# Both rope products of a projection half in one VectorE operation of 1024 columns, with the sine reached by a backward step

## The chip, the cores and the metric

The kernel runs on the 8 cores of one Trainium2 chip, as one program for all of them; each core computes 2048 of the 16384 tokens. The metric is the time of the slowest core, in microseconds (us). Before the change it was 1009.27 us, the median of 3 runs (1008.91 to 1009.8).

One property of this program decides how its runs have to be compared. In most runs some pairs of cores (0 and 1, 2 and 3, 4 and 5, 6 and 7) run with TensorE at a granted clock of 0.81 (46.1 to 209.0 us in the profiled run before); the other pairs don't, also on the same die (in the profiled run before, cores 0 and 1 ended at 1005 us with the stretch, cores 2 and 3 at 989 to 991 us without). Which pairs it is changes from run to run. A core that has this stretch ends about 16 us later and has a mean clock near 0.957, one that doesn't has about 0.983. The profiled runs show the stretch itself; in the other runs I tell the two kinds apart by the mean clock. I call them **lower-clock** and **higher-clock** cores. The time of a run is that of its lower-clock cores, unless there are none, which happened in 9 of the 40 later runs of the kernel before (993 to 995 us, where nearly all others had 1006 to 1010). Those runs make ratios of whole runs noisy (they also make an ordinary run of 1008.5 us count as slow, being over 1.5% above the fastest), so the experiments below compare lower-clock cores with lower-clock cores and higher-clock cores with higher-clock ones, always with the kernel before in the same rounds on the same chip. Cores over 1040 us, in the few runs of a much slower state (1042 to 1169 us, mean clock 0.806 to 0.929), are left out.

## The reference, cut to what matters

```python
def apply_rope(t):                       # t: (B, S, H, 64)
    ...                                  # cos, sin by position and by 32 frequencies
    t1, t2 = tf[..., :half], tf[..., half:]
    out = jnp.concatenate([t1 * cos - t2 * sin, t2 * cos + t1 * sin], axis=-1)

def reference(x, ...):
    h = rms_norm(x, g_pre_mix[l])
    proj = h @ w_in[l]                   # q, k, v, pool input, gates
    q = apply_rope(q)
    k = apply_rope(k)
    # dilated window attention in three groups of heads, pooling branch, gated merge,
    # output projection, then a SwiGLU feed-forward layer
```

Rope needs four products for each projection: with a = t1 and b = t2, it needs a·cos and b·sin (subtracted), and a·sin and b·cos (added).

## The kernel before

Weights are permuted so that all first halves of four heads come out of one group of eight matmuls and all second halves out of the next. They land in two neighbouring PSUM banks. VectorE makes the products with a table from SBUF; GpSimd adds or subtracts and writes bf16.

```python
tabs = P.ring("tab", [128, 2, 512], F32, ...)        # row 0 cosine, row 1 sine; two buffers
rt = P.ring("rt", [128, 2, 512], F32, ..., False)    # products; two buffers
any2, fill2 = pairs([0, 2, 4, 6]), pairs([4, 6])     # pairs of PSUM banks
# ... cut ...
def rope(ring, wa, wb, rhs, tn, dst_a, dst_b, view, n=512, t0=0):
    tb = tab(tn)
    b = ring.new()
    cos, sin = tb[:, 0, t0:t0 + n], tb[:, 1, t0:t0 + n]
    mm8(b[:, 0, 0:n], wa, rhs)
    mm8(b[:, 1, 0:n], wb, rhs)
    for dst, fa, fb, op in ((dst_a, cos, sin, ALU.subtract), (dst_b, sin, cos, ALU.add)):
        t = rt.new()
        dve.tensor_tensor(out=t[:, 0, 0:n], in0=b[:, 0, 0:n], in1=fa, op=ALU.mult)
        dve.tensor_tensor(out=t[:, 1, 0:n], in0=b[:, 1, 0:n], in1=fb, op=ALU.mult)
        pool.tensor_tensor(out=dst, in0=view(t[:, 0, 0:n]), in1=view(t[:, 1, 0:n]), op=op)
```

The kernel doesn't fix the order of its instructions by hand. It records every operation as a node with its dependencies, then a list scheduler orders the five engines' queues with the kernel's own prices, and only then are the instructions and semaphore waits written out. The prices that matter here:

```python
def op_cost(eng, method, outs, ins, kw):             # us
    # ... cut ...
    if eng == "vector":
        # ... cut: reciprocal, and all-bf16 operations ...
        return 0.12 + (0.00170 if strided else 0.00110) * n
```

So a product of 512 columns is priced at 0.683 us and one of 1024 at 1.246 us. There are 30 projections with rope, 29 of 512 columns and one of 128: 120 products before.

The softmax here doesn't subtract the row's maximum and nothing guards it: scores larger than these inputs give would overflow.

## Time and profile before

| | before |
|---|---|
| time, median | 1009.27 us |
| profiled run, by core | 988.9 to 1007.7 us |
| PE busy (slowest core) | 93% |
| VectorE busy | 379.4 us, 509 instructions |
| products (the tiles rt) | 120, from 27 to 319 us |

In the profile, PE is TensorE, DVE is VectorE, ACT is ScalarE, POOL is GpSimd. The first lines are the cores' spans and mean granted clocks.

```profile
core 2: 990.8 us, clock 0.984
...
core 5: 1007.7 us, clock 0.957
```

Core 2 is a higher-clock core here, core 5 a lower-clock one. From the page of core 5: busy time, share and number of instructions of each engine, and below it the granted TensorE clock in 40 slices of 25 us.

```profile
PE 941.1 (93%) x5520; PEld 483.0 (48%) x5520; DVE 379.4 (38%) x509; ACT 349.2 (35%) x558; POOL 364.9 (36%) x366
...
PEclk9888888899999999999999999999999999999997
```

TensorE is the limit of the whole, and VectorE matters only where TensorE waits for it. The groups of products follow: operation, output and inputs, shape, count, then the busy time, the mean length of one in ns, and how long the engine was idle before them and for whom.

```profile
L608 DVE TENSOR_TENSOR rt_72_114<-ps,tab_71_113 128x512 f32<-128x512 f32 x30 | 20.3, 685 | 24.7 <-PE ps L608 22.5 <-POOL q_1_65_107 L608 1.5 <-POOL k_34_76 L608 0.6
...
L608 DVE TENSOR_TENSOR rt_73_115<-ps,tab_71_113 128x512 f32<-128x512 f32 x30 | 19.8, 681 | 3.7 <-POOL q_1_65_107 L608 2.5 <-POOL k_34_76 L608 0.7 <-POOL q_33_75 L608 0.5
...
L608 DVE TENSOR_TENSOR rt_72_114<-ps,tab_70_112 128x512 f32<-128x512 f32 x28 | 18.7, 686 | 16.7 <-PE ps L608 9.4 <-ACT PT_75_117 L608 2.9 <-POOL k_34_76 L608 2.6
L608 DVE TENSOR_TENSOR rt_73_115<-ps,tab_70_112 128x512 f32<-128x512 f32 x28 | 18.3, 679 | 1.7 <-POOL q_33_75 L608 1.0 <-POOL k_34_76 L608 0.7
```

How a projection runs shows in the timeline (start, length, engine, operation, count; in brackets the idle time before it):

```profile
143.81 2.01 PE L610 MATMUL ps<-hTh_69,wk_67_109 128*128 128x512 bf16 x7
...
144.16 0.69 DVE L608 TENSOR_TENSOR rt_72_114<-ps,tab_71_113 128x512 f32<-128x512 f32 x1 [2.53 <-PE ps L608]
...
144.77 0.68 DVE L608 TENSOR_TENSOR rt_73_115<-ps,tab_71_113 128x512 f32<-128x512 f32 x1
...
145.65 0.44 PE L608 MATMUL ps<-hTh_69,wk_67_109 128*128 128x512 bf16 x1
...
146.20 0.69 DVE L608 TENSOR_TENSOR rt_72_114<-ps,tab_71_113 128x512 f32<-128x512 f32 x1 [0.74 <-PE ps L608]
...
146.80 0.68 DVE L608 TENSOR_TENSOR rt_73_115<-ps,tab_71_113 128x512 f32<-128x512 f32 x1
147.03 2.17 POOL L608 TENSOR_TENSOR k_0_61_103<-rt_72_114 128x512 bf16<-128x512 f32 x1 [4.79 <-DVE rt_72_114 L608]
```

The second half's matmuls run from 143.81 to 146.09. In that time VectorE already makes both products of the first half. Two products in a row start 0.60 us apart although each lasts 0.68 us or more. GpSimd begins 0.94 us after the second half ended, and the last read of the bank pair ends at 147.48, 1.39 us after it.

The table by stretches (start:end, length, busy time of PE, its weight loads, DVE, ACT, POOL with counts, granted clock, DMA share, GB/s) of core 5:

```profile
46.00:205.00 159.00, 153.12 (x1223) 103.62 (x1221) 90.34 (x134) 93.69 (x157) 78.05 (x58) 0.81 0.44 111
205.00:285.00 80.00, 74.61 (x708) 47.86 (x707) 57.83 (x80) 40.09 (x62) 49.45 (x37) 0.99 0.19 41
285.00:300.00 15.00, 11.49 (x108) 6.04 (x105) 10.36 (x17) 6.15 (x8) 8.79 (x7) 0.89 0.36 53
300.00:330.00 30.00, 26.49 (x152) 12.07 (x153) 21.07 (x26) 12.23 (x15) 22.82 (x22) 0.94 0.43 65
```

The clock of 0.81 is the long stretch of the lower-clock cores.

### The profile page before, as it was taken

Reading aid. Unit: us, or ns where it says so; the run is one execution under the profiler, and the core shown is the slowest. Engines: PE = TensorE matmul, PEld = TensorE weight load, DVE = VectorE, ACT = ScalarE, POOL = GpSimd, SP = SyncE. Lnnn points to the kernel's source line nnn. Section 1 sums busy time; section 2 is a strip of 40 time slices with the busy share of each in tenths; the row PEclk is TensorE's granted clock in tenths of the full one; section 3 lists DMA queues with packets and bytes.
Section 4 is the critical chain, followed back from the end, with each engine's and each line's share of the span. In section 5 each row is a group of like instructions: output and inputs, shape, how many; then the busy total and the mean of one; then the engine's idle time right before and its main releaser. Section 6 shows DMA issues by size and latency. Waiting matters only on the chain.

```text
span 1007.7 us, 15210 instructions; the slowest of 8 cores (988.9 to 1007.7 us)
## 1 busy us (share of the span) xinstructions
PE 941.1 (93%) x5520; PEld 483.0 (48%) x5520; DVE 379.4 (38%) x509; ACT 349.2 (35%) x558; POOL 364.9 (36%) x366
## 2 busy tenths in 40 slices
PE   2789999998988999999899999999999999999992
PEld 1356686665743444444444444444444444444441
DVE  5667625658767434332544121121112112111111
ACT  4696425653634434422774111111111111110110
POOL 1526643455757352533885111111322000001332
PEclk9888888899999999999999999999999999999997
DMA  8967710140024633640877665663234344430321
GB/s 233 286 168 230 165 36 2 43 84 2 23 54 62 117 53 61 158 74 14 265 239 207 113 116 106 108 124 79 89 126 125 66 81 83 66 61 21 105 84 42
DMA packets 30777, 105.01 MB, mean 104 GB/s; under 512 B 3952, under 2 KB 3952, under 8 KB 30704
## 3 DMA queue, kind: packets, MB, share of 16 engines
q0 software_dynamic: 14432, 45.65, 26.9%
q1 hardware_dynamic: 15984, 58.33, 17.3%
q8 instruction: 45, 0.74, 0.3%
q14 instruction: 28, 0.23, 0.1%
q10 hardware_dynamic: 288, 0.06, 0.0%
HBM read 132.90 MB, written 16.78 MB: 149 GB/s over the span
## 4 chain that ended last, share of the span: by engine, by line
PE 82%; DVE 4%; POOL 4%; issue 4%; ACT 2%; DMA 1%; SPq 0%; POOLq 0%; DVEq 0%; ACTq 0%
PE ps L610 73%; PE ps L608 10%; DMA xst_40_82<-xo 1%; DVE PT_75_117 L608 1%; ACT xsb_53_95 L608 1%; POOL x1b_103_145 L608 1%; POOL x1b_102_144 L608 1%; DVE PT_74_116 L608 1%; DVE rt_73_115 L608 1%; POOL x1b_101_143 L608 0%; DVE zT_134 L608 0%; POOL x1b_104_146 L608 0%; POOL q_33_75 L608 0%; DVE val_67 L608 0%; DVE x1b_102_144 L608 0%
## 5 line engine op out<-in xcount | busy, mean ns | idle before, releaser
L610 PE MATMUL ps<-wdna_155,ffT_154 128*128 128x512 bf16 x512 | 115.7, 379 | 0.0
L610 PE MATMUL ps<-hT_68,wgu_109_151 128*128 128x512 bf16 x420 | 100.4, 379 | 0.0
L610 PE MATMUL ps<-hT_68,wgu_110_152 128*128 128x512 bf16 x420 | 100.4, 379 | 0.0
L610 PE MATMUL ps<-hT_68,wgu_111_153 128*128 128x512 bf16 x392 | 93.7, 379 | 0.0
L610 PEld LDWEIGHTS ps<-wdna_155,ffT_154 128*128 128x128 bf16 x512 | 50.1, 98 | 60.4
L610 PEld LDWEIGHTS ps<-hT_68,wgu_109_151 128*128 128x128 bf16 x420 | 41.0, 98 | 49.3
L610 PEld LDWEIGHTS ps<-hT_68,wgu_110_152 128*128 128x128 bf16 x420 | 41.0, 98 | 49.1
L610 PEld LDWEIGHTS ps<-hT_68,wgu_111_153 128*128 128x128 bf16 x392 | 38.3, 98 | 46.3
L610 PE MATMUL ps<-hT_68,wgs_76_118 128*128 128x512 bf16 x224 | 53.6, 379 | 1.9 <-ACT yp_87_129 L608 1.2
L610 PE MATMUL ps<-hT_68,wgs_77_119 128*128 128x512 bf16 x224 | 53.6, 379 | 0.4 <-DVE zT_134 L608 0.4
L608 DVE TENSOR_TENSOR ffT_154<-ps,sa_115_157 128x512 bf16<-128x512 f32 x30 | 20.7, 691 | 79.6 <-PE ps L608 79.6
L608 DVE TENSOR_TENSOR ffT_154<-ps,sa_116_158 128x512 bf16<-128x512 f32 x29 | 20.1, 691 | 78.8 <-PE ps L608 78.8
L608 DVE TENSOR_TENSOR ffT_154<-ps,sa_117_159 128x512 bf16<-128x512 f32 x29 | 20.0, 691 | 76.3 <-PE ps L608 76.3
L608 ACT ACTIVATE junkd_107_149<-ps 128x1024 bf16<-128x1024 f32 x19 | 19.3, 1017 | 77.0 <-PE ps L608 76.8
L608 ACT ACTIVATE sa_115_157<-ps 128x512 f32<-128x512 f32 x30 | 17.9, 598 | 80.2 <-PE ps L608 80.2
L608 ACT ACTIVATE sa_116_158<-ps 128x512 f32<-128x512 f32 x29 | 17.3, 597 | 80.9 <-PE ps L608 80.9
L608 ACT ACTIVATE sa_117_159<-ps 128x512 f32<-128x512 f32 x29 | 17.3, 597 | 78.0 <-PE ps L608 78.0
L608 DVE SCALAR_TENSOR_TENSOR tg_81_123<-tg_81_123,ps 128x512 f32<-128x512 f32 x32 | 22.0, 688 | 47.8 <-ACT tg_81_123 L608 44.7
L610 PE MATMUL ps<-wdnb_156,ffT_154 128*128 128x512 bf16 x160 | 39.8, 379 | 0.0
L608 POOL DMA_DIRECT2D wgu_109_151<-wgu x15 | 8.0, 536 | 81.3 <-PE ps L608 81.3
L608 POOL DMA_DIRECT2D wgu_110_152<-wgu x15 | 8.2, 544 | 80.7 <-PE ps L608 80.7
L608 ACT ACTIVATE junkd_108_150<-ps 128x1024 bf16<-128x1024 f32 x13 | 13.2, 1018 | 69.4 <-PE ps L608 69.4
(496 smaller groups left out, 1867.9 us busy)
## 6 DMA issues: line engine op xcount, KB each, us to landing
wgu_109_151<-wgu POOLq DMA_DIRECT2D x15, 512.0 KB, 5.7
wgu_110_152<-wgu POOLq DMA_DIRECT2D x15, 512.0 KB, 5.7
wgu_111_153<-wgu POOLq DMA_DIRECT2D x14, 512.0 KB, 5.4
wgs_76_118<-wg POOLq DMA_DIRECT2D x8, 512.0 KB, 6.0
wgs_77_119<-wg POOLq DMA_DIRECT2D x8, 512.0 KB, 5.2
wdna_155<-wdn POOLq DMA_DIRECT2D x8, 512.0 KB, 8.3
tab_70_112<-tab SPq DMA_DIRECT2D x6, 512.0 KB, 6.4
tab_71_113<-tab SPq DMA_DIRECT2D x6, 512.0 KB, 4.6
```

What stands on the lines that cost most here:

```text
L608: e.ops.append(lambda q, m=method, a=a, k=k, s=sem.sem, v=step: getattr(q, m)(*a, **k).then_inc(s, v))
L610: e.ops.append(lambda q, m=method, a=a, k=k: getattr(q, m)(*a, **k))
```

## The change

The intent is fewer VectorE instructions: one operation multiplies both halves. For the first output the table is read as cosine, sine; for the second it starts at the sine and steps back by 512 columns to the cosine.

```diff
-        cos, sin = tb[:, 0, t0:t0 + n], tb[:, 1, t0:t0 + n]
+        f = tb[:, 0, t0:t0 + n]
         mm8(b[:, 0, 0:n], wa, rhs)
         mm8(b[:, 1, 0:n], wb, rhs)
-        for dst, fa, fb, op in ((dst_a, cos, sin, ALU.subtract), (dst_b, sin, cos, ALU.add)):
+        for dst, swap, op in ((dst_a, False, ALU.subtract), (dst_b, True, ALU.add)):
             t = rt.new()
-            dve.tensor_tensor(out=t[:, 0, 0:n], in0=b[:, 0, 0:n], in1=fa, op=ALU.mult)
-            dve.tensor_tensor(out=t[:, 1, 0:n], in0=b[:, 1, 0:n], in1=fb, op=ALU.mult)
+
+            tf = tb[:, 1, t0:t0 + n].fap([(-512, 2), (1, n)]) if swap else f.fap([(512, 2), (1, n)])
+            dve.tensor_tensor(out=t[:, :, 0:n], in0=b[:, :, 0:n], in1=tf, op=ALU.mult)
             pool.tensor_tensor(out=dst, in0=view(t[:, 0, 0:n]), in1=view(t[:, 1, 0:n]), op=op)
```

## The prediction

> **What bounds the kernel now.** TensorE. The page gives PE 93% of the span, DVE 38%, ACT 35%, POOL 36%; the chain of waits is 82% PE, 4% DVE, 4% POOL. After about 330 us PE has no gap that matters and the changed operations are gone: the groups of the product tiles (rt) run from 27 to 319 us. So the change can act only in the first third. The table by stretches shows PE 89 of 100 us busy in 25–125, about 99 in 125–225, 88 in 225–325. The list of PE's waits in 125–325 sums to 13 us, of which the rope products own 2.7 us. By core, from about 30 to 205 us the slow cores run at a granted clock of 0.81; cores 2 and 3 mostly do not, and finish 16 us earlier. So for half of the affected stretch the slowest cores are bound by a slow PE, with slack elsewhere.
>
> **What it removes.** 120 products (116 of 512 columns, 4 of 128) become 60. A 512-column product lasts 691 ns alone; back to back, starts are 0.60 us apart. [...] The trace has a 1024-column eviction from PSUM at 1221 ns, with starts 1.14 us apart. So a pair falls from 1.37 to 1.22 us of summed durations, but its occupancy only from 1.20 to 1.14 us. Over 58 large pairs: 8 us of durations, about 4 us of VectorE time (DVE busy 379 to about 372).
>
> **What it adds.** A merged product needs both matmul halves. Now the two products of the first half run while PE makes the second (starts at 144.16 and 144.77; the other two at 146.20 and 146.80). After the second half, GpSimd will start 0.5 us later than now, and the PSUM pair is released 1.1 us later (2.46 instead of 1.38 us after that half). VectorE idled for PE before a product 27 times. It also becomes less divisible: a mask multiplication (PT) may sit behind 1.2 us. I expect no new contention with GpSimd from the products (their durations do not spread now); mask multiplications do spread (0.68 to 3.4 us), and will collide at other moments.
>
> **Critical path.** Where VectorE is saturated (225–250 us: 91% busy) the shorter pair helps: 8 pairs per block, 0.5–1 us. The later release costs only where PE wants those banks. I expect 1–3 us gained, 1–3 us lost. The greater term: the program orders its instructions by its own cost model, so new lengths and a new dependency reshuffle all queues of the first 330 us; I allow ±6 us for that.
>
> **Prediction:** 1008 us, 80% range 999 to 1017. Faster by over 2%: 0.04; within 2%: 0.92; slower by over 2%: 0.04.
>
> **What the profile would show.** Right: 58 products of 2x512 columns at 1.20–1.24 us, about 71 us in all; POOL's work near 365 us; PE's work unchanged; unchanged length after 330 us; the same 0.81 stretch; more VectorE idle before products, waiting for PE. Wrong: a merged product well over 1.24 us (the backward step or two banks cost something); PE waits on rt growing by over 5 us; the stretch up to 330 us changing by over 8 us.
>
> **What would make it wrong.** The clock: a longer or shorter 0.81 stretch on the slowest cores, up to 16 us either way. Or an unlucky order of mask multiplications against GpSimd's long operations in 200–325 us.

The sum stands on the trace of before: the median lengths of the two products of a pair, 691 and 680 ns, make the 1.37 us, and the eviction of 1221 ns the 1.22 us. 58 pairs times 0.15 us give 8.7 us of durations (recorded as 8), and 58 times the 0.06 us between the distances of starts (1.20 and 1.14 us) 3.5 us of VectorE time (recorded as about 4). The clock records put the 0.81 stretch of the slow cores from 46 to 209 us, not from about 30 to 205.

On the collisions that it speaks of, the trace of before shows this (core 5): the 17 mask multiplications that ran beside no GpSimd operation took 0.675 to 0.694 us; the 31 that ran beside one took 0.674 to 3.425, 16 of them 0.79 or more. No product took more than 0.693 us, though 77 of the 120 ran beside one.

## The result, and the profile after

The time fell to 1006.44 us (median of 4, 1004.74 to 1007.01) against 1009.13 us (median of 4) of the kernel before. The ratio is 0.9971, with a 95% interval from 0.9952 to 0.9991. That is less than 2%; the interval says that the small gain is there. Ratios of this kind are the mean time of one kernel's fast runs over that of the other's of the same rounds, so they aren't quite the ratio of the medians.

| | before | after |
|---|---|---|
| time, median | 1009.13 us | 1006.44 us |
| lower-clock cores, mean (same chip, later rounds) | 1006.1 us (30 cores) | 1003.8 us (22 cores) |
| higher-clock cores, mean (same rounds) | 990.5 us (58 cores) | 990.3 us (22 cores) |
| VectorE busy, profiled core | 379.4 us | 373.1 us |
| summed lengths of the products, by groups | 78.2 us | 71.3 us |

The gain shows on the lower-clock cores only: 2.3 us there, 0.2 us on the others. (The section on the pairs that stood next to each other comes back to why.)

The cores and the page of the slowest, after:

```profile
core 0: 987.9 us, clock 0.985
...
core 5: 1005.5 us, clock 0.958
```

```profile
PE 940.3 (94%) x5520; PEld 482.4 (48%) x5520; DVE 373.1 (37%) x449; ACT 345.8 (34%) x556; POOL 369.8 (37%) x366
...
PEclk9887888899999999999999999999999999999996
```

The products after:

```profile
L608 DVE TENSOR_TENSOR rt_72_114<-ps,tab_71_113 128x1024 f32<-128x1024 f32 x15 | 18.3, 1221 | 20.5 <-PE ps L608 19.0 <-POOL k_34_76 L608 1.3
L608 DVE TENSOR_TENSOR rt_73_115<-ps,tab_71_113 128x1024 f32<-128x1024 f32 x15 | 18.2, 1215 | 1.3 <-POOL k_34_76 L608 1.3
L608 DVE TENSOR_TENSOR rt_72_114<-ps,tab_70_112 128x1024 f32<-128x1024 f32 x14 | 17.0, 1215 | 16.2 <-PE ps L608 15.9 <-DMA tab_70_112<-tab 0.2
L608 DVE TENSOR_TENSOR rt_73_115<-ps,tab_70_112 128x1024 f32<-128x1024 f32 x14 | 17.0, 1214 | 0.1
```

A merged product lasts 1214 to 1221 ns in the mean, in all four groups, and none of the 58 large ones lasts more than 1226 ns. Half of them step forward and half backward, so the backward step costs nothing that shows. Reading across two banks costs nothing that shows either, measured against the two products of one bank each: one merged product is shorter than both together (1.22 against 1.37 us). The same projection as before, after the change:

```profile
142.32 2.01 PE L610 MATMUL ps<-hTh_69,wk_67_109 128*128 128x512 bf16 x7
...
144.16 0.44 PE L608 MATMUL ps<-hTh_69,wk_67_109 128*128 128x512 bf16 x1
...
144.77 1.23 DVE L608 TENSOR_TENSOR rt_72_114<-ps,tab_71_113 128x1024 f32<-128x1024 f32 x1 [4.50 <-PE ps L608]
...
145.91 1.21 DVE L608 TENSOR_TENSOR rt_73_115<-ps,tab_71_113 128x1024 f32<-128x1024 f32 x1
...
146.14 2.21 POOL L608 TENSOR_TENSOR k_0_61_103<-rt_72_114 128x512 bf16<-128x512 f32 x1 [5.19 <-DVE rt_72_114 L608]
```

The matmuls end at 144.60. VectorE had nothing to do while the second half ran. GpSimd begins 1.54 us after the matmuls' end, where it was 0.94 us, and the bank pair's last read ends at 147.12, 2.52 us after it, where it was 1.39. Two merged products start 1.14 us apart: the pair occupies VectorE for 1.14 us where it took 1.20.

The table by stretches of core 5, after:

```profile
46.00:205.00 159.00, 154.88 (x1238) 105.34 (x1237) 85.57 (x100) 93.35 (x160) 79.60 (x57) 0.81 0.48 116
205.00:285.00 80.00, 74.06 (x720) 45.49 (x719) 59.30 (x70) 39.53 (x57) 52.99 (x38) 0.99 0.26 41
285.00:300.00 15.00, 14.14 (x116) 9.15 (x114) 11.67 (x13) 4.65 (x9) 9.90 (x11) 1.00 0.46 85
300.00:330.00 30.00, 26.74 (x183) 12.78 (x182) 20.16 (x21) 14.22 (x21) 23.09 (x22) 1.00 0.62 99
```

From 285 to 330 us the granted clock is now 1.00 where it was 0.89 and 0.94. The length from the first matmul of the feed-forward layer to the end is 475 us in both (532.6 to 1007.7, and 530.3 to 1005.5), so all of the gain was made before it. Between the two kernels the order of TensorE's queue itself has changed, so a comparison place by place isn't possible; that is what the experiments are for.

### The profile page after: what moved, and what is told of

It reads as the page before. It is cut to its first block, busy times and chain, and to the rows that moved or that the text cites. A ratio compares the mean times of both kernels' runs of the same rounds, so it can differ in the third digit from the quotient of the medians.

```text
span 1005.5 us, 15161 instructions; the slowest of 8 cores (987.9 to 1005.5 us)
## 1 busy us (share of the span) xinstructions
PE 940.3 (94%) x5520; PEld 482.4 (48%) x5520; DVE 373.1 (37%) x449; ACT 345.8 (34%) x556; POOL 369.8 (37%) x366
## 4 chain that ended last, share of the span: by engine, by line
PE 82%; issue 5%; DVE 4%; POOL 4%; ACT 2%; DMA 2%; POOLq 0%; DVEq 0%; ACTq 0%; SPq 0%
PE ps L610 72%; PE ps L608 10%; DMA wgs_77_119<-wg 1%; DMA xst_37_79<-xo 1%; POOL x1b_101_143 L608 1%; DVE rt_73_115 L608 1%; ACT xsb_53_95 L608 1%; POOL x1b_103_145 L608 1%; POOL x1b_102_144 L608 1%; POOL x1b_104_146 L608 0%; DVE PT_75_117 L608 0%; DVE PT_74_116 L608 0%; DVE den_135 L608 0%; DVE rt_72_114 L608 0%; DVE zT_134 L608 0%
## 5 line engine op out<-in xcount | busy, mean ns | idle before, releaser
L608 ACT ACTIVATE junkd_107_149<-ps 128x1024 bf16<-128x1024 f32 x19 | 19.3, 1017 | 77.0 <-PE ps L608 76.9
L608 POOL DMA_DIRECT2D wgu_109_151<-wgu x15 | 8.1, 540 | 81.3 <-PE ps L608 81.3
L608 POOL DMA_DIRECT2D wgu_110_152<-wgu x15 | 8.1, 542 | 80.7 <-PE ps L608 80.7
L608 POOL DMA_DIRECT2D wgu_111_153<-wgu x14 | 7.4, 531 | 81.2 <-PE ps L608 74.9
```

The lines of the kernel that those rows point to most:

```text
L608: e.ops.append(lambda q, m=method, a=a, k=k, s=sem.sem, v=step: getattr(q, m)(*a, **k).then_inc(s, v))
```

## The experiments

Two theories. **A**: the cheaper operation made the gain. **B**: the operation is worth little, later products cost something, and the gain is in the new order of the queues that the kernel's own scheduler came to when a price and a dependency changed. To tell them apart, the order has to be held still while the operation changes, and the other way round. All kernels gave correct results. Medians of whole runs are in the text; the table at the end has the two classes of cores.

### The merged products in the order of before

```diff
+def join_pairs(prog):               # called after the scheduler, before the instructions are written out
+    pos = {n.idx: i for i, n in enumerate(prog.order)}
+    gone = {}
+    for x, y, items in prog.pairs:  # the two products of a pair; items: the one of 1024 columns
+        keep, drop = (x, y) if pos[x.idx] > pos[y.idx] else (y, x)
+        gone[drop.idx] = keep.idx
+        keep.deps |= drop.deps
+        # ... cut ...
+        keep.items = items or drop.items + keep.items
+    # ... cut: drop leaves the order, and whoever waited for it waits for keep ...
```

The queues of TensorE, ScalarE, GpSimd and the DMA queue are those of before, instruction by instruction.

> The merged products in the order of before: every engine's instruction sequence is that of before, except that each pair of products is one 1024-column product at the place of the later one. Theory A (the cheaper operation made the gain): the ratio to before is as that of the change, about 0.997 (-3 us). Theory B (the gain is the new order that the program's own cost model chose, the operation itself is worth nothing): 1.000, or up to 1.002 because every product waits for both matmul halves. I lean to B: 1.000 +- 0.001. In the profile, DVE busy about 372 us, as in the changed kernel, under either theory.

Measured: median 1013.77 us. Lower-clock cores 1011.4 us (before 1006.1), higher-clock cores 992.3 us (before 990.5). The products were 1218 ns long and took 69.6 us. Both theories missed: I leaned to 1.000, and the change in a frozen order is a clear loss of 5.3 and 1.8 us. Theory A, as it was put, falls. Note that the frozen order was made for early products: it is no neutral ground for late ones.

### The order of the change, with two products instead of one

```diff
-            dve.tensor_tensor(out=t[:, :, 0:n], in0=b[:, :, 0:n], in1=tf, op=ALU.mult)
+            with dve.group() as g:           # one node, two instructions
+                [dve.tensor_tensor(out=t[:, h, 0:n], in0=b[:, h, 0:n], in1=tf[:, h, :], op=ALU.mult) for h in range(2)]
+            g.cost = 0.12 + 0.0011 * 2 * n   # the price of the merged one: same order
```

> The order of the changed kernel on every engine, with each merged product issued as two products of 512 columns, one directly behind the other, both waiting for both halves. Theory A: the gain is lost, ratio to before about 1.000 (VectorE has 58 x 0.06 = 3.5 us more to do than in the changed kernel, and 120 products again). Theory B: the gain stays, 0.997 to 0.998, about 1006 to 1007 us; DVE busy back near 379 us.

Measured: median 1007.74 us; lower-clock cores 1004.7 us, higher-clock cores 989.9 us, against 1003.8 and 990.3 of the changed kernel in the same rounds. With 120 instructions again, most of the gain on the lower-clock cores is still there. In this order the merged operation is worth 0.9 us on one class and −0.4 on the other.

### The order of before, with both products late

As the first experiment, but the pair stays two products of 512 columns at the place of the later one.

```diff
-            P.pairs.append((x, y, [('tensor_tensor', (), dict(out=t[:, :, 0:n], in0=b[:, :, 0:n], in1=tf, op=ALU.mult))]))
+            P.pairs.append((x, y, None))     # so keep.items is drop.items + keep.items
```

> The order of before, 120 products of 512 columns as before, but both products of a pair issued together at the place of the later one, so that no product runs before both matmul halves are done. It differs from before by the later start alone, and from the merged products in the order of before by the operation alone. If the later start costs something: 1.001 to 1.003 (+1 to +3 us). If it falls into slack: 1.000 +- 0.0007. I expect 1.001. The run with merged products in the order of before should then be faster than this one by at most 0.001 under theory B, and by about 0.003 under theory A.

Measured: median 1015.44 us; lower-clock cores 1012.9 us, higher-clock cores 994.7 us. The later start alone costs 6.8 and 4.2 us in the order of before, two to four times what I expected. The shorter operation (the first experiment against this one) then gives 1.5 and 2.4 us back.

Because TensorE's queue is the same in before and here, each of its matmuls can be compared with itself. On lower-clock cores (medians of the five with complete records) this kernel is 3.3 us behind at 56 us, keeps about that distance to 209 us (2.7), is 3.9 behind at 231 us, 4.0 at 304, 7.4 at 339 and 8.3 at the end of the profiled run. The loss is made in a few places, not spread over 30 projections.

### The changed kernel again

> The changed kernel once more, as the reference on the same chip and in the same rounds: ratio 0.997 (0.996 to 0.998), 1006 us, whatever theory.

Measured: median 1006.05 us (before 1008.44 us in the same rounds); lower-clock cores 1003.8, higher-clock cores 990.3 us. The ratio of fast runs that came with it, 1.0044 (0.9968 to 1.0119), is not usable: two of the runs of before had no lower-clock core at all (993 and 995 us) and were counted with the fast ones. By class of cores the change gains as in its first runs.

### Only the order moves: four prices

The next four kernels keep all instructions and dependencies and change a price in the scheduler's cost model.

```diff
 # the kernel before, products priced at half a merged one (0.623 us instead of 0.683)
+            x.cost = y.cost = 0.5 * (0.12 + 0.0011 * 2 * n)
 # the changed kernel, merged products priced as two (1.366 us instead of 1.246)
+            x.cost = 2 * (0.12 + 0.0011 * n)
 # both kernels, all full-rate VectorE operations priced by the measured distance of two starts
-        return 0.12 + (0.00170 if strided else 0.00110) * n
+        return 0.067 + (0.00170 if strided else 0.00104) * n
```

> The kernel before, with the same 120 products of 512 columns and the same dependencies; only the price that the program's own cost model puts on a product is lowered from 0.683 to 0.623 us, half of what it puts on a merged one. So only the order of the queues moves. Theory B (the order is a draw whose scatter is as large as the whole effect): the mean span of the cores at the lower clock moves by 1 to 6 us from the 1006 us of before, in either direction. Theory A: it stays within 1 us.

Measured: median 1022.45 us; lower-clock cores 1018.6 us, higher-clock cores 1002.7 us. A price 9% lower on 120 operations, with not one instruction different, costs 12 us (before in these rounds: 1006.6 and 990.1). More than the 1 to 6 us that I expected.

> The changed kernel with the same 60 merged products and dependencies; only the price in the cost model is raised from 1.246 to 1.366 us, what two products cost there. Theory B: the mean span of the cores at the lower clock moves by 1 to 6 us from the 1004 us of the changed kernel, more likely up than down, and the change may then look worse than before. Theory A: it stays within 1 us of 1004.

Measured: median 1017.9 us; lower-clock cores 1014.9 us, higher-clock cores 998.3 us: 11 and 8 us slower than the changed kernel, and slower than before.

> The changed kernel, with the price of every VectorE operation at the full rate set to the measured distance of two starts (0.067 us plus 1.04 ns a column, so 0.60 us for 512 and 1.13 us for 1024 columns). If the order suffers from a wrong price: 3 to 6 us faster than the changed kernel (lower-clock cores below 1001 us). If the order is a draw: anywhere from 1000 to 1010 us on those cores. I expect the latter, about 1004.

Measured: median 1021.26 us; lower-clock cores 1019.4 us, higher-clock cores 1002.0 us. Truer prices gave no better order; I had expected about 1004.

> The kernel before with the same measured price for VectorE. With the run of the changed kernel at this price it is a second pair of before and after under another order. Theory A: the changed kernel again gains 2 to 3 us over this one. Theory B: the difference of the pair is anything from -5 to +5 us.

Measured: median 1019.89 us; lower-clock cores 1018.1 us, higher-clock cores 1003.2 us.

Read as pairs, the change is worth something different under every price (lower-clock cores, higher-clock cores):

| price | before | changed | change |
|---|---|---|---|
| 0.683 a product of 512, 1.366 a merged one | 1006.1, 990.5 | 1014.9, 998.3 | +8.8, +7.8 |
| 0.623 a product of 512, 1.246 a merged one | 1018.6, 1002.7 | 1003.8, 990.3 | −14.8, −12.4 |
| measured distance of starts | 1018.1, 1003.2 | 1019.4, 1002.0 | +1.3, −1.2 |
| as shipped (0.683, and 1.246) | 1006.1, 990.5 | 1003.8, 990.3 | −2.3, −0.2 |

The shipped pair compares two good draws. Neither was topped by any redraw here. That can be luck, or the prices were chosen with the order in view; no run here tells.

### Merging only the pairs that stood next to each other

If late products are the loss, then merging only pairs that were adjacent on VectorE anyway (35 of 60 in the trace: 33 of 512 columns, which the expectation counts, and both of 128) should keep the gain and avoid the loss.

```diff
+    rank = {n.idx: i for i, n in enumerate(n for n in prog.order if n.eng is prog.dve)}
+    near = [p for p in prog.pairs if abs(rank[p[0].idx] - rank[p[1].idx]) == 1]
-    for x, y, items in prog.pairs:
+    for x, y, items in near:
```

> The order of before on every engine; of the 60 pairs only those 33 whose two products already stood next to each other on VectorE are merged, the other 27 (where the first product ran while TensorE made the second half) stay as they were. If the loss of the merged products in the order of before (+5 us on the lower-clock cores) came from products made late, it is nearly gone here, and what is left is the worth of the shorter operation: lower-clock cores 1004 to 1006 us, higher-clock cores 989 to 991 us (before: 1006.1 and 990.5). If the loss had another cause (the wide operation itself, its reading of two banks), about half of it stays: 1008 to 1009 us.

Measured: median 1012.29 us; lower-clock cores 1009.3 us, higher-clock cores 990.9 us (before 1006.6 and 990.3). On the higher-clock cores as expected; on the lower-clock cores a loss of 2.7 us that I had not expected, and half of the full one. The number is that of the other branch, a loss by the wide operation itself, but that branch doesn't fit: in the same order, merged products were 1.5 and 2.4 us faster than two late ones. By place (one core, the only one with complete records, against the median of before), the loss at 56 us is gone (0.3 us). This kernel falls back by 1.4 us between 231 and 260 us, by 0.8 between 285 and 300 and by 2.0 between 304 and 339. What happens there led to the most useful finding. These are TensorE's pauses in the kernel before on core 5, and then here on core 7, both lower-clock cores (idle time in brackets):

```profile
288.29 0.59 PE L610 MATMUL ps<-q_0_64_106,k_0_58_100 32*128 32x256 bf16 x7 [0.68 <-ACT PT_74_116 L608]
...
290.16 0.29 PE L610 MATMUL ps<-q_0_64_106,k_2_63_105 32*128 32x128 bf16 x4 [1.27 <-ACT PT_75_117 L608]
...
291.43 0.55 PE L610 MATMUL ps<-PT_74_116,v_56_98 128*128 128x128 bf16 x5 [0.65 <-DVE PT_74_116 L608]
...
309.73 3.06 PE L610 MATMUL ps<-hT_68,wk_67_109 128*128 128x512 bf16 x7 [2.32 <-DVE rt_73_115 L608]
```

```profile
289.83 0.59 PE L610 MATMUL ps<-q,k 32*128 32x256 bf16 x7 [0.68 <-ACT PT L608]
...
291.99 1.01 PE L610 MATMUL ps<-q,k 32*128 32x128 bf16 x15 [1.54 <-ACT PT L608]
...
311.75 2.97 PE L610 MATMUL ps<-hT,wk 128*128 128x512 bf16 x7 [2.60 <-DVE rt L608]
```

The pauses are about the same. But the table by stretches of that core has a lower clock from 285 to 300 us, 0.77 where before had 0.89:

```profile
285.00:300.00 15.00, 12.78 (x123) 7.29 (x123) 9.93 (x15) 6.28 (x7) 6.82 (x7) 0.77 0.25 37
300.00:330.00 30.00, 25.66 (x149) 11.63 (x147) 19.49 (x23) 12.34 (x15) 24.14 (x22) 0.94 0.47 65
```

The clock records of the trace say why: TensorE was granted half its clock for 6.8 us from 291.5 us on, where before it was 3.4 us. The other two places go the same way: here half clock begins at 243.7 and at 312.0 us as well, and of the six lower-clock cores of before only one has it at each (core 6 at 243.9, core 5 at 309.1). In all kernels these stretches last 3.4 us or a multiple of it (3.413, 6.827 and 10.240 us in before and after), and they come with a cluster of pauses or with one long one. On every core all these stretches between 45 and 960 us begin on one grid of 3.413 us: between two of them lie 13.653 us of full clock on core 5 of before and 44.373 us on its cores 3 and 6, 4 and 13 steps of the grid. A window, in what follows, is one step of that grid. I count, in all profiled runs, the windows between 45 and 400 us on cores with complete matmul records (the ends of matmuls are modelled, so the shares are approximate). Half clock begins 242 times: TensorE had been idle for 36 to 100% of the window before (median 63%), and for all of it 11 times. Of the windows not at half clock already, none that was idle for 59% or more went without it. In before and after alone it begins 18 times, after windows idle for 44 to 80%, and none idle for 53% or more went without it. The single pauses can be shorter than a window: in the kernel before, those of 0.68, 1.27 and 0.65 us above, within 4 us, were followed by 3.4 us at 0.50, the single one of 2.32 us by another 3.4, and here 0.68 and 1.54 us by 6.8 us.

The kernel before holds a comparison: one program, and nearly the same pause, which falls otherwise into the window. Before the matmuls at 309 us TensorE pauses for 2.3 us on all its lower-clock cores. On core 0 a window ends 1.59 us into the pause, which makes 47% of that window idle, and the clock stays full (as on the other four); on core 5 it ends 1.74 us into it, which makes 51%, and half clock follows. Core 0, to be set against the last line of core 5 above and its row for 300 to 330 us (0.94):

```profile
309.10 1.67 PE L610 MATMUL ps<-hT_68,wk_67_109 128*128 128x512 bf16 x7 [2.31 <-DVE rt_73_115 L608]
...
300.00:330.00 30.00, 26.62 (x161) 12.40 (x160) 21.08 (x26) 12.83 (x16) 23.41 (x22) 1.00 0.52 75
```

The same seven matmuls take 3.06 us instead of 1.67, and core 5 falls 1.4 us behind core 0 there. By arithmetic a stretch of 3.4 us takes away up to 1.7 us of TensorE's work. So nearly the same pause, followed by half clock on one core and not on the other, costs 1.4 us more here. Near one half the share of the window, as I count it, doesn't tell alone: in after, half clock followed a window idle for 50% (core 7, from 266.3 us), and none followed five windows idle for 51 to 52% (cores 0, 1, 5 and 7).

The mean time at half clock per core, between 45 and 960 us, in the profiled run of each kernel (lower-clock cores); the loss that it makes, less that of before; and the excess of the span of the same cores over before. The loss counts half of the time, or 0.31 of it inside the 0.81 stretch, where half clock takes away only that much:

| kernel | at half clock | its loss, over before | excess of the span |
|---|---|---|---|
| before | 4.6 us | – | – (1005.9 us) |
| changed (first run) | 3.4 us | −1.0 us | −2.2 us |
| order of before, adjacent pairs merged | 13.7 us | 4.6 us | 4.0 us |
| order of before, all merged | 11.1 us | 2.6 us | 5.5 us |
| order of before, both late | 13.7 us | 3.9 us | 7.7 us |
| before, lower price | 18.8 us | 6.5 us | 11.2 us |
| changed, higher price | 23.9 us | 8.4 us | 8.8 us |
| changed, measured prices | 17.1 us | 5.0 us | 13.2 us |
| before, measured prices | 20.5 us | 6.7 us | 12.2 us |

Half-clock stretches account for about four tenths to all of what the bad orders lose (for one of them, for 0.6 us more than all); the rest I put down to the pauses themselves. The same count speaks to why the change gains on one class only: on the higher-clock cores its loss at half clock is 0.9 us larger than in before (two cores each), on the lower-clock ones 1.0 us smaller. Without it, the change gains about 1 us on either class (1.2 and 1.0). No run here set the clock by hand: the comparison of cores above shows the cost of one stretch, and the table is an account by arithmetic, not a proof of cause for each kernel. The worst order (before with the lower price, core 6) shows the kind of pause, three of them with 2.15 to 2.89 us, waiting for products and masks:

```profile
309.78 1.95 PE L610 MATMUL ps<-hT,wk 128*128 128x512 bf16 x7 [2.15 <-DVE rt L608]
...
321.06 0.62 PE L610 MATMUL ps<-PT,v 128*128 128x256 bf16 x3 [2.84 <-DVE PT L608]
...
336.07 0.91 PE L610 MATMUL ps<-PT,v 128*128 128x128 bf16 x7 [2.89 <-DVE PT L608]
```

### The order of the change, with an early first product

```diff
 # ... cut: the pair and its two products are noted in P.pairs ...
-        mm8(b[:, 1, 0:n], wb, rhs)
+        late = mm8(b[:, 1, 0:n], wb, rhs)
+def split_pairs(prog):               # called after the scheduler
+    for g, late, items in prog.pairs:
+        first = prog.node(g.eng)
+        first.items, g.items = items         # two products of 512 columns
+        first.outs, first.ins = g.outs, g.ins
+        first.deps, first.vts = g.deps - {late.idx}, g.vts
+        prog.order.insert(prog.order.index(g), first)
```

> The order of the changed kernel on every engine; each merged product is two of 512 columns at the same place, and the first waits for its own matmul half only. It differs from the earlier run of two products in this order (1004.7 lower, 989.9 higher clock) by that wait alone. If the new order is one in which late products cost nothing: the same within 1 us. If late products cost here too: 1 to 3 us faster than 1004.7 and faster than the changed kernel (1003.8). I expect 0 to 1 us faster, because the order was made for late products.

Measured: median 1005.74 us; lower-clock cores 1002.4 us, higher-clock cores 989.4 us. That is 2.3 and 0.5 us better than the two late products in this order, and 1.4 and 0.9 us better than the merged ones of the earlier rounds: so late products cost here too, but a third or less of what they cost in the order of before. It is the best median that I measured with lower-clock cores, without one merged operation, though by less than the cores of one kernel scatter (standard deviation 1.6 us). The 2.3 us compare runs on two chips.

### The merged products in a second frozen order

The order of the run with the cheaper price for the unmerged products, and all pairs merged in it by the edit of the first experiment.

> The order of the run with the cheaper price for the unmerged products (1018.6 us lower, 1002.7 higher clock), with all pairs merged at the place of the later product. A second order in which the change is made without moving the queues. If the loss in a frozen order is a property of the change: +2 to +6 us on the lower-clock cores, 1021 to 1024 us, +1 to +3 on the others. If it was peculiar to the order of before: between -2 and +1 us.

Measured: median 1023.1 us; lower-clock cores 1028.9 us (4 cores), higher-clock cores 1009.6 us, against 1018.6 and 1002.7 us in that order without merging. So in a second frozen order the change loses too, 10 and 7 us, more than expected. (The lower-clock cores are those of two runs only.) On the higher-clock cores the clock does not explain it: both have 20.5 us at half clock. TensorE's waits between 20 and 400 us do, for the most part: on each of cores 0 to 3 of the profiled runs, those for products (rt) grow from 7.8 to 12.1 us, those for mask multiplications (PT) from 8.1 to 10.0, and all together from 39-41 to 45-46 us.

### Both first products ahead

The early version, with the two products of the first half ahead of the two of the second where they are neighbours.

```diff
 # ... cut: p is the node in front of g on VectorE, lead its early product ...
+        if p.idx in lead and lead[p.idx][1] is late and all(pos[d] < pos[p.idx] for d in need):
+            place.setdefault(p.idx, []).append(lead[g.idx][0])   # ahead of the neighbour p, same projection
+        else:
+            place.setdefault(g.idx, []).insert(0, lead[g.idx][0])
```

> The order of the changed kernel, 120 products of 512 columns, each waiting for its own half only; where both products of a projection stood next to each other, both of the first half come first, as in the kernel before, so that the bank pair is given back about 1.1 us sooner than with merged products. If late products still cost something in the new order: lower-clock cores 1000.5 to 1002 us (1002.4 with the plain early start, 1003.8 with merged products), median of the whole 1003 to 1005 us, the best version so far. If their cost is used up: 1002.4 within 1 us. I expect 1002 and 989. The count of half-clock stretches of 3.4 us per core should go along: where a core ends 1.7 us later or more than its like, it has one more of them.

Measured: median 1006.71 us; lower-clock cores 1003.9 us, higher-clock cores 989.7 us (before 1006.0 and 990.3). A miss: giving the bank pair back earlier brought nothing over the plain early start, and is even with the merged products. What is left of late products in the new order is within the scatter. It is also a second measurement of the early start, and a smaller one: 0.8 and 0.2 us better than the two late products, not 2.3 and 0.5. The other part of the expectation held: in the profiled run the two lower-clock cores without half clock after 45 us end at 1001.0 and 1002.3 us, the four with 6.8 us of it at 1003.0 to 1005.1.

### All of them

Means of cores, us, with the number of cores in parentheses; before of the same rounds: 1006.0 to 1006.6 and 990.1 to 990.5.

| order | products | lower clock | higher clock |
|---|---|---|---|
| before | two, early (the kernel before) | 1006.1 (30) | 990.5 (58) |
| before | two, late | 1012.9 (22) | 994.7 (26) |
| before | merged where neighbours | 1009.3 (26) | 990.9 (34) |
| before | merged | 1011.4 (18) | 992.3 (26) |
| of the change | merged (the change) | 1003.8 (22) | 990.3 (22) |
| of the change | two, late | 1004.7 (20) | 989.9 (28) |
| of the change | two, first early | 1002.4 (22) | 989.4 (22) |
| of the change | two, interleaved | 1003.9 (24) | 989.7 (32) |
| before, lower price | two, early | 1018.6 (6) | 1002.7 (38) |
| before, lower price | merged | 1028.9 (4) | 1009.6 (40) |
| change, higher price | merged | 1014.9 (16) | 998.3 (28) |
| change, measured prices | merged | 1019.4 (10) | 1002.0 (22) |
| before, measured prices | two, early | 1018.1 (10) | 1003.2 (22) |

## Why the prediction was right

The time, 1006.44 us, lies inside the range of 999 to 1017 and 1.6 us from the 1008 predicted. A forecast of no change at all would have been inside it too, so the number alone tests little. Point by point:

- **Where the change can act.** Right: the feed-forward part keeps its 475 us, and the last product starts at 303 us where it started at 319.
- **What the operation costs.** Right. The forecast goes by the eviction of 1024 columns in the trace of before, 1221 ns, and expects 1.20 to 1.24 us; measured were 1214 to 1221 ns. VectorE's busy time went to 373 us (predicted 372), the products to 71.3 us (predicted 71), and the distance of starts is the 1.14 us predicted. The useful figure was that distance, not the length: the lengths promise 8 us, the occupancy about 4.
- **What waiting for both halves costs locally.** Right in size: GpSimd begins 0.60 us later (predicted 0.5), the bank pair is released 1.13 us later (predicted 1.1).
- **"1–3 us gained, 1–3 us lost."** The gain was right in the order of before, 1.5 and 2.4 us; in that of the change it was 0.9 and −0.4. The loss was too small: 6.8 and 4.2 us in the order of before. In the order of the change, waiting for both halves costs 2.3 and 0.5 us by one run, 0.8 and 0.2 by the other. The sign to watch, TensorE's waits for products growing by over 5 us, did not show: 2.7 us before and 3.1 after, between 125 and 325 us.
- **"The greater term: ... reshuffle all queues ...; I allow ±6 us for that."** The kind was right, and it is what made the result: from all merged in the order of before to the change, the order alone gives 7.6 and 2.0 us. On the lower-clock cores the sum is +6.8 (late) −1.5 (operation) −7.6 (order) = −2.3 us, on the higher-clock cores +4.2 −2.4 −2.0 = −0.2 us. The split depends on the way taken. By way of the order of the change with two products, the first early, it is −3.7 (order) +2.3 (late) −0.9 (operation) and −1.1 +0.5 +0.4: there the order is worth half as much. The order matters more to late products than to early ones. The size was too small by half: four price changes moved the two classes of cores by 8 to 16 us, all upward. The range held because the shipped order happened to be a good one, not because the term was small.
- **The clock.** The 0.81 stretch stayed (162 us before, 158 us after on the lower-clock cores, on four of which half clock interrupts it for 3.4 us), as predicted. The clock effect that does move with the order is another: the half-clock stretches of 3.4 us, which I had before me as 0.89 and 0.94 and did not ask about.

What stays open: why these two orders are better than the four redrawn ones. Both orders of the shipped kernels have few half-clock stretches, but no run here made an order with that aim. And the second frozen order loses 7 us on higher-clock cores at equal half-clock time; its waits say for what TensorE stood still longer, but not why so much more than in the first.

## What to carry to other kernels

In a kernel whose queues are ordered by a scheduler, test an edit twice: in the frozen order of before, which tells what the edit is worth in an order made for the old kernel, and in its own new order; a small gain or loss of the second alone says little, because a price changed by a tenth moved this kernel by more than 1%. Merging two operations over two matmul halves saved only what the distances of starts allow (0.06 us a pair: 0.60 us twice against 1.14; the lengths promise 0.15) and gave up the overlap with the second half (the bank pair came free 1.13 us later); I would try it only where VectorE is behind already, an opinion that no run here shows. Where TensorE is the limit, count the long pauses and those that come in clusters: here a stretch of 3.4 us at half clock came on top of their own length after windows of the 3.413 us grid that were idle for 36 to 100%, but after none of five that were idle for 51 to 52% in the changed kernel.
